# A gating layer's ungated half by seven block products instead of eight, with the block sums made by accumulating loads

## The chip, the core and the metric

The kernel runs on one core of one Trainium2 chip. The metric is the device time of one execution in microseconds (us). TensorE (PE in the profile) multiplies matrices and transposes tiles, VectorE (DVE) and ScalarE (ACT) do element-wise work, GpSimd (POOL) does a little of it. Transfers between the large memory and the on-chip memory (SBUF) are issued from queues: the one of SyncE (SP), the one of ACT, and the one of POOL. Matmul results land in eight accumulation banks (PSUM).

## The reference

Two layers work on a stream `x` of 512 tokens x 1024 features. Layer 0 mixes tokens by chunked attention, layer 1 by a spatial gating layer; each is followed by a feed-forward block of width 4096. All of it is in float32. The part that the change is about is layer 1's mixer:

```python
SG_FF = 6 * D_MODEL          # D_MODEL = 1024
SG_HALF = SG_FF // 2         # 3072
SG_GROUPS, SG_WINDOW, CHUNK = 8, 128, 64

def chunked_spatial_gating(h, w_in, v_gain, w_s, b_s, w_out):
    B, S, _ = h.shape
    nw = S // SG_WINDOW
    z = jax.nn.gelu(h @ w_in, approximate=False)
    u, v = jnp.split(z, 2, axis=-1)
    v = rms_norm(v, v_gain).reshape(B, nw, SG_WINDOW, SG_GROUPS, SG_HALF // SG_GROUPS)
    chunk_id = jnp.arange(SG_WINDOW) // CHUNK
    mask = chunk_id[:, None] >= chunk_id[None, :]
    w = jnp.where(mask[None], w_s, 0.0).astype(v.dtype)
    vm = jnp.einsum('gij,bnjgc->bnigc', w, v) + b_s.T[None, None, :, :, None]
    return (u * vm.reshape(B, S, SG_HALF)) @ w_out

def squared_relu_mlp(h, w1, w2):
    return jnp.square(jax.nn.relu(h @ w1)) @ w2

# per layer: x = x + g1 * mixer(norm(x)); x = x + g2 * squared_relu_mlp(norm(x), w1, w2)
```

In the text `v` is the gated half's input to the mixing ("gate"), `u` the ungated half, and `w_out` the closing product.

## The kernel before

**Products in three passes.** Every float32 operand is split into a high and a low part in a reduced format (`Split`, `wload`: ACT copies the high part, DVE subtracts it for the low part), and `mm3` multiplies high by high, high by low, low by high. So a product over 128 rows of the contraction, 128 tokens and 512 columns takes three matmuls of 128x512.

**Seven products.** `seven(left, src, y)` multiplies a 512 x 1024 activation by a 1024 x 1024 weight as two by two blocks with seven block products instead of eight. Each of its seven steps has four parts: `load` (weight blocks by SP), `right` (the weight blocks' sums on DVE in `sub`, at line 631, and the splits), `left` (sums of activation blocks on DVE, `comb`, and their split) and `mult` (the matmuls, 2 token tiles x 4 k x 3 for one block product; sums over products stay in the accumulation banks or go through `y.put`). `Spent` frees the activation operands after use; `Kept` keeps them for several products in a row. `Run` executes a list of such steps, loads `ll + lp` steps and splits `lp` steps ahead of the matmuls. It is used in the feed-forward layers (`down_steps` there, three of four quarters) and for two thirds of the gate (`Gate(1)`, `Gate(2)`).

**The gating layer, in order.** The first third of the gate is done plainly by `gate_tile` (column blocks 0 and 1, eight products), the rest by two sevens. Each block of v after its Gelu is written to a buffer `vd` in large memory by POOL's queue (`v_store`), and its sums of squares go to `vss`. Then the mixing weights are transposed (line 1495), and `u_block(cb)` runs for six blocks of 512 columns of the ungated half: for each of four token tiles 8 k x 3 matmuls, the Gelu out of the bank, then the mixing of that tile: v is read back, scaled by row scale and gain (L1533), split (L1535, L1536), mixed by two groups' weights (`mm3`, 128 to 384 columns each), biased and multiplied into u (L1549), transposed (L1554) and split again (L1559, L1560). `b_down` multiplies each gated block of 512 columns by its rows of `w_out` and sums in `y` (`Sum`); the last two blocks go through `project_last`, which also adds the residual.

**The last projection.** `project_last` works tile by tile: `merge(t)` scales the sum so far by g and adds the residual that was loaded from `xsg` (L505 to L507); two halves of 512 columns are multiplied; `add_residual` (L424, L425) adds each; `rows(t)` norms the row tile (L304 to L306); `cols(t - 1)`, in the middle of the next tile's second half, transposes the normed tile (L315) for the feed-forward layer. `merge(t)` for t > 0 is issued behind the norm of the tile before (`issue_after(normed[0].ins)`).

**Order.** Outside stretches under `in_order`, which keep PE's instructions as written, a planner orders each engine's instructions by costs of its own. Buffers come from a pool of 49 slots (`Slots`), taken in the order in which they were freed; a load into a slot waits for its last reader. Background work (`bg`) adds up the modulation rows for later stages on DVE from weights loaded on SP.

Of the kernel before, what the change touches and what calls it, by code (L numbers as in the profile page):

```python
# [16 lines left out]
P = 128  # L17
# [35 lines left out]
def trunk_kernel(  # L53
# [378 lines left out]
    def project_last(actT, src, g, rows, cols=None, after=None, merge=None, spent=None):  # L432
# [3 lines left out]
        ws = [ahead.pop(hf) if hf in ahead else wload(src[:, hf * 512:hf * 512 + 512], n) for hf in range(2)]  # L436
        if after is not None:
            ahead["w"] = after()
        for t in range(NT):
# [3 lines left out]
            for hf in range(2):  # L443
                w = ws[hf][0]
                nc_ = 256 if cols is None and (t, hf) == (NT - 1, 1) else 512
                for c0 in range(0, 512, nc_):
                    ps, pi = bank()
                    if hf == 1 and t > 0 and cols is not None:
                        gemm_tok(actT, w[:n // 2], t, ps, 0, n - 1)
                        cols(t - 1)  # L450
# [11 lines left out]
            if cols is not None:  # L462
                rows(t)

# [24 lines left out]
    class Sum:  # L489
# [5 lines left out]
        def merge(self, xs, g):  # L495
            merged = set()

            def merge(t):
# [4 lines left out]
                xt[t], xid[t] = self.y[t], self.ids[t]  # L503
                raw, done = raw_tile([P, D])
# [7 lines left out]
        def put(self, t, hf, ps):  # L512
# [3 lines left out]
            if (t, hf) in self.seen:  # L516
                V.tensor_tensor(dst, ps, dst, ALU.add)  # L517
# [4 lines left out]
    class Spent:  # L522
# [13 lines left out]
        def prep(self, m):  # L536
            if m == 0:
                self.ab = self.blocks()
            elif m == 2:
                self.ab["x"] = SL.get([P, 4, 256], F32)  # L540
                self.comb("x", (1, 0), (1, 1), ALU.add)
            elif m == 3:
                self.comb("x", "x", (0, 0), ALU.subtract)
            elif m == 4:
                self.comb((0, 1), (0, 1), "x", ALU.subtract)
# [3 lines left out]
            if m == 5:  # L549
                self.also()  # L550
            self.spend(*((), (), (), (), ("x", (0, 1)), ((0, 0), (1, 0)), ((1, 1),))[m])

        def also(self):
            pass
# [4 lines left out]
    class Kept(Spent):  # L559
# [11 lines left out]
        def prep(self, m):  # L571
            if m in self.op:
                return
            self.comb(*{
                2: ("x", (1, 0), (1, 1), ALU.add), 3: ("x", "x", (0, 0), ALU.subtract),
                4: ((0, 1), (0, 1), "x", ALU.subtract), 5: ((0, 0), (0, 0), (1, 0), ALU.subtract),
            }[m])
            self.op[m] = Split(self.ab[("x", "x", (0, 1), (0, 0))[m - 2]][0], [P, 4, 256])
            self.spend(*((), (), ("x", (0, 1)), ((0, 0), (1, 0), (1, 1)))[m - 2])
# [5 lines left out]

        def done(self, m):
            pass

        def only_blocks(self):

            for m in (2, 3, 4, 5):
                self.op.pop(m).free()
            return self.rows()

        def free(self):
            for x in self.op.values():
                x.free()
# [18 lines left out]
    def seven(left, src, y):  # L616
# [3 lines left out]
        def load(i, j):  # L620
            raw[i, j] = []
            for s_ in range(2):
                t, n = SL.get([P, 2, 512], F32)
                r0 = i * 512 + s_ * 256
                SP.dma_start(t, src[r0:r0 + 256, j * 512:j * 512 + 512].rearrange("(k p) n -> p k n", p=P))
                raw[i, j].append((t, n))

        def sub(d, a, b):

            for x, y_, z in zip(raw[d], raw[a], raw[b]):  # L630
                V.tensor_tensor(x[0], y_[0], z[0], ALU.subtract)  # L631

        def drop(*blocks):
            for b in blocks:
                SL.free(*[n for _, n in raw.pop(b)])

        def right(m):
            if m == 2:
                sub((0, 0), (0, 1), (0, 0))
            elif m == 3:  # L640
                sub((0, 0), (1, 1), (0, 0))
            elif m == 5:
                sub((0, 1), (1, 1), (0, 1))
            elif m == 6:
                sub((1, 0), (1, 0), (0, 0))
# [1010 lines left out]
```

## Time and profile before

| | before |
|---|---|
| median of 3 runs (lowest to highest) | 1410.66 us (1408.36 to 1410.92) |
| profiled execution: time | 1412.96 us |
| profiled execution: span of its instructions | 1411.2 us |
| mean granted TensorE clock | 0.993 |
| DMA traffic | 221.51 MB, mean 157 GB/s |
| hardware queues' share of the DMA engines, software queue's (POOL) | 45.9%, 1.1% |

The profile is of one execution. Busy time is the time in which an engine worked on instructions; matmuls are pipelined, so a busy PE need not be at its peak. A row of instructions names line, engine, operation, output and inputs, shape and count, then busy time and mean time of one, then the idle time before them and what ended it. "Landing" is the time from a transfer's issue to its data being there.

### The profile page before, as it was taken

The page shows a single profiled execution, that of the slowest core. Times are in us where ns is not written, and L with a number is a line of the kernel's source. Part 1 is how long each engine was busy: PE and PEld are TensorE (multiplying, and loading weights), DVE is VectorE, ACT ScalarE, POOL GpSimd, SP SyncE. Part 2 cuts the span into 40 slices and gives each one's busy share as a digit, 9 for nine tenths or more (in the row PEclk, how much of TensorE's full clock was granted, in tenths as well). Part 3 has the DMA queues.
Part 4 walks back from the last instruction along what each step waited for, and adds up shares of the span by engine and source line. Part 5 has one row for each costly group of instructions (what it writes and reads, how often), then busy time and mean ns, then how long its engine had stood idle before and what let it go on. Part 6 is the DMA issues. An engine that isn't in the chain of part 4 may idle for free.

```text
span 1411.2 us, 18916 instructions
## 1 busy us (share of the span) xinstructions
PE 1386.7 (98%) x7202; PEld 1185.5 (84%) x7202; DVE 1020.9 (72%) x1493; ACT 713.5 (51%) x1231; POOL 15.7 (1%) x46
## 2 busy tenths in 40 slices
PE   8999999899999999999999999999999999999998
PEld 7898888789888888888888888888889988888887
DVE  6889889676667887776995745665677377776883
ACT  6537567655464544537587443233445355453630
POOL 0000000000000000000000000000000000000000
PEclk8999999999999999999999999999999999999999
DMA  9656466573254361356347434435437225242151
GB/s 373 240 144 211 147 194 173 201 264 110 90 169 144 119 224 60 118 197 252 134 147 254 167 106 164 163 127 164 142 113 269 75 87 182 63 147 90 31 164 60
DMA packets 85627, 221.51 MB, mean 157 GB/s; under 512 B 7960, under 2 KB 9376, under 8 KB 85536
## 3 DMA queue, kind: packets, MB, share of 16 engines
q1 hardware_dynamic: 83808, 214.01, 45.9%
q0 software_dynamic: 1728, 6.29, 1.1%
q8 instruction: 56, 0.92, 0.3%
q14 instruction: 35, 0.29, 0.1%
HBM read 197.21 MB, written 14.68 MB: 150 GB/s over the span
## 4 chain that ended last, share of the span: by engine, by line
PE 88%; DMA 6%; DVE 3%; ACT 2%; issue 1%; SPq 0%; POOL 0%; ACTq 0%; POOLq 0%; DVEq 0%
PE p L92 85%; DMA s<-in_ada_w 2%; DMA s<-in_ffn_w 1%; DMA s<-in_a_w_in 1%; DMA s<-in_a_w_out 1%; DMA s<-s 1%; PE p L1554 1%; PE p L1228 1%; PE p L315 1%; DVE s L484 0%; PE p L1139 0%; PE p L920 0%; DVE s L951 0%; ACT s L483 0%; PE p L207 0%
## 5 line engine op out<-in xcount | busy, mean ns | idle before, releaser
L92 PE MATMUL p<-s,s 128*128 128x512 f32 (+2 forms) x6568 | 1323.8, 361 | 9.5 <-DVE nm L1190 2.7
L92 PEld LDWEIGHTS p<-s,s 128*128 128x128 f32 x6568 | 1109.4, 189 | 196.0 <-DVE nm L1190 4.3
L484 DVE TENSOR_TENSOR s<-s,s 128x1024 fp32r<-128x1024 f32 x234 | 280.5, 1222 | 119.1 <-ACT s L483 56.0
L483 ACT CAST s<-s 128x1024 fp32r<-128x1024 f32 x234 | 241.2, 1051 | 166.0 <-PE p L92 109.9
L389 DVE TENSOR_TENSOR s<-s,s 128x1024 fp32r<-128x1024 f32 x80 | 96.7, 1223 | 62.2 <-ACT s L388 50.7
L388 ACT CAST s<-s 128x1024 fp32r<-128x1024 f32 x80 | 83.4, 1052 | 93.8 <-DMA s<-in_b_w_out 34.1
L631 DVE TENSOR_TENSOR s<-s,s 128x1024 f32<-128x1024 f32 x64 | 77.7, 1222 | 33.0 <-DMA s<-in_ffn_w 32.6
L739 ACT ACTIVATE r<-p 128x512 f32<-128x512 f32 x64 | 38.1, 595 | 116.6 <-PE p L92 116.5
L194 DVE SCALAR_TENSOR_TENSOR s<-s,cs,s 128x1024 f32<-128x1024 f32 x70 | 89.7, 1281 | 8.7 <-DMA s<-in_ada_w 7.7
L517 DVE TENSOR_TENSOR s<-p,s 128x512 f32<-128x512 f32 x104 | 70.4, 686 | 19.2 <-PE p L92 18.0
L745 ACT ACTIVATE s<-r 128x256 f32<-128x256 f32 (+1 forms) x112 | 45.0, 443 | 1.2
L424 DVE TENSOR_TENSOR tr<-p,s 128x512 f32<-128x512 f32 (+1 forms) x33 | 22.0, 671 | 30.6 <-PE p L92 30.2
L1195 ACT ACTIVATE s<-s,nm 128x128 f32<-128x128 f32 (+3 forms) x64 | 36.0, 564 | 7.4 <-DVE nm L1190 5.9
L1559 ACT CAST s<-p 128x256 fp32r<-128x256 f32 x48 | 17.7, 370 | 35.5 <-PE p L1554 27.0
L530 DVE TENSOR_TENSOR s<-s,s 128x1024 f32<-128x1024 f32 x28 | 33.6, 1221 | 1.0 <-PE p L92 0.9
L304 ACT ACTIVATE s<-s 128x512 f32<-128x512 f32 x24 | 15.3, 638 | 36.0 <-DVE s L425 34.9
L1233 DVE TENSOR_TENSOR s<-p,s 128x512 fp32r<-128x512 f32 (+3 forms) x64 | 29.3, 484 | 4.0 <-ACT s L1232 3.6
L1560 DVE TENSOR_TENSOR s<-p,s 128x256 fp32r<-128x256 f32 x48 | 20.1, 419 | 16.3 <-ACT s L1559 16.3
L1190 DVE CUSTOM_DVE_ANT_0 s<-p,s 128x128 f32<-128x128 f32 (+3 forms) x64 | 29.6, 485 | 0.9 <-PE p L92 0.8
L1535 ACT CAST s<-s 128x512 fp32r<-128x512 f32 x24 | 14.8, 621 | 27.8 <-DVE s L1533 12.9
L1228 PE MATMUL p<-ident,s 128*128 128x128 f32 x160 | 24.6, 275 | 4.1 <-ACT sq L1310 2.4
L1232 ACT CAST s<-p 128x512 fp32r<-128x512 f32 (+3 forms) x64 | 25.1, 426 | 6.6 <-PE p L1228 5.5
(141 smaller groups left out, 760.9 us busy)
## 6 DMA issues: line engine op xcount, KB each, us to landing
s<-in_ffn_w SPq DMA_DIRECT2D x128, 512.0 KB, 4.5
s<-in_ada_w SPq DMA_DIRECT2D x96, 512.0 KB, 4.9
s<-in_b_w_in SPq DMA_DIRECT2D x48, 512.0 KB, 5.0
s<-in_b_w_out SPq DMA_DIRECT2D x24, 512.0 KB, 4.8
s<-in_a_w_in SPq DMA_DIRECT2D x22, 512.0 KB, 5.2
s<-s SPq DMA_DIRECT2D x64, 128.0 KB, 3.6
vd<-s POOLq DMA_DIRECT2D x12, 512.0 KB, 3.2
s<-vd SPq DMA_DIRECT2D x12, 512.0 KB, 3.4
```

What stands on the lines that cost most here:

```text
L92: T.matmul(ps, lhsT, rhs, start=start, stop=stop, skip_group_check=more)
L194: V.scalar_tensor_tensor(acc, r, ck, acc, ALU.mult, ALU.add)
L388: A.copy(hi, raw)
L389: engs[len(ids) // 2 % len(engs)].tensor_tensor(lo, raw, f32(hi), ALU.subtract)
L483: A.copy(self.hi, raw)
L484: mark[0] = V.tensor_tensor(self.lo, raw, f32(self.hi), ALU.subtract)
L517: V.tensor_tensor(dst, ps, dst, ALU.add)
L631: V.tensor_tensor(x[0], y_[0], z[0], ALU.subtract)
L739: A.activation(r, ps, AF.Relu)
L745: A.activation(d, v, AF.Square)
L1195: A.activation(pt[it], pt[it], AF.Exp, bias=nm[:, it:it + 1], scale=-1.0, accum_out=sm[:, it:it + 1])
L1228: T.transpose(ps[:, it * P:(it + 1) * P], b["pt"][it][:, jt * P:(jt + 1) * P], ident)
```

## The change

It touches four things.

- **Ungated half.** `u_block` goes. The ungated half becomes three sevens over 1024 columns (`mix_steps`, class `Mix`), which use the kept activation operands of the gate. A finished 128 x 512 piece of u gets its Gelu in `Mix.put`; its mixing is put on a list and issued two half steps later (five for the very first) by `flush`. The gated tiles are gathered in blocks of 512 columns x 256 tokens (`gated`) and split as a whole (`take_parts`).
- **Sums by loads.** The seven products take another set of sums, in which each weight operand is a running sum of blocks: x = B00, then + B01, + B11, + B10, and y = B11, then + B01. A block is loaded by SP; the further ones are added onto it in SBUF by an accumulating load from POOL's queue (`grow`) once the split of the operand before has read it. In gate and ungated half (`apart`) the first operand B00 has a buffer of its own, and x is loaded again and grown early.
- **Half steps.** Each of the seven steps becomes two, over 256 weight rows each. `Run` now looks 4 + 4 half steps ahead (before: 3 + 3 whole steps in the feed-forward layers, 2 + 2 in the gate).
- **Closing product.** `down_steps` in the gating layer multiplies 1024 rows of `w_out` in eight half steps, second 512 rows ahead of the first, four token tiles at a time in four banks. Order: ungated third 0, its closing product, ungated thirds 1 and 2, closing product 1, then the last projection for third 2. There the residual is added by an accumulating load from POOL's queue (`late`).

Besides, `v_store` is issued from ACT's queue, and the mixing weights are prepared ahead of the run.

```diff
-        def put(self, t, hf, ps):
+        def put(self, t, hf, ps, op=ALU.add, whole=True):
...
+                if late:
+                    V.tensor_tensor(xt[t], xt[t], g, ALU.mult)
+                    G.dma_start(xt[t], xs[t], accum_op=ALU.add)
+                    return
                 raw, done = raw_tile([P, D])
                 SP.dma_start(raw, xs[t])
                 V.tensor_tensor(xt[t], xt[t], g, ALU.mult)
...
-    def seven(left, src, y):
+    def seven(left, src, y, apart=False):
...
+        def load(name, i, j, s_):
+            raw[name, s_] = t, n = SL.get([P, 2, 512], F32)
+            SP.dma_start(t, block(i, j, s_))
+
+        def grow(i, j, name, s_):
+            G.dma_start(raw[name, s_][0], block(i, j, s_), accum_op=ALU.add)
+
+        def right(m, name, add, s_):
+            t, n = raw[name, s_]
+            op[m, s_] = Split(t, [P, 2, 512])
+            if add is None:
+                SL.free(n)
+            else:
+                grow(*add, name, s_)
...
         plan = (
-            (True, ((0, 0),), False),
-            (True, ((0, 0),), True),
-            (True, ((1, 1),), False),
-            (False, ((0, 1),), False),
-            (False, ((0, 1),), True),
-            (False, ((1, 0), (1, 1)), True),
-            (True, ((1, 0),), True),
+            (0, ("f" if apart else "x", 0, 0), ("f", None) if apart else ("x", (0, 1)), ("z", True, ((0, 0, add, False),), False)),
+            (1, ("z", 1, 0), ("z", None), ("y", True, ((0, 0, add, False),), True)),
+            (2, None, ("x", (1, 1)), ("v", True, ((1, 1, add, False),), False)),
+            (4, ("y", 1, 1), ("y", (0, 1)), ("v", False, ((0, 1, add, False),), True)),
+            (3, None, ("x", (1, 0)), ("z", False, ((0, 1, sub, False),), False)),
+            (5, None, ("y", None), ("z", False, ((1, 1, sub, False),), False)),
+            (6, None, ("x", None), ("z", False, ((1, 0, add, True),), True)),
         )
-        blocks = ((0, 0), (1, 0), (0, 1), (1, 1))
+        def loads(m, b, s_):
+            if b:
+                load(*b, s_)
+            if apart and m == 1:
+                load("x", 0, 0, s_)
+                grow(0, 1, "x", s_)
...
-        run = Run(steps, 3, 3)
+        run = Run(steps, 4, 4)
...
-        G.dma_start(vd[cb, b], v.rearrange("p t n -> p (t n)"))
+        A.dma_start(vd[cb, b], v.rearrange("p t n -> p (t n)"))
...
+        def put(self, t, hf, ps, op, whole):
+            if (hf, t // 2) not in self.u:
+                self.u[hf, t // 2] = SL.get([P, 2, 512], F32)
+            dst = self.u[hf, t // 2][0][:, t % 2, :]
+            if not whole and (t, hf) not in self.seen:
+                self.seen.add((t, hf))
+                A.copy(dst, ps)
+                return
+            if not whole:
+                V.tensor_tensor(dst, dst, ps, op)
+            A.activation(dst, ps if whole else dst, AF.Gelu)
+            late = 5 if (self.p, hf, t // 2) == (0, 0, 0) else 2
+            later.append((now[0] + late, lambda: self.mix(t, hf, dst)))
...
+        def mult(n):
+            hf, j, o = n // 4, 1 - n // 2 % 2, n % 2
+            w = op.pop(n)
+            for t in range(NT):
+                if n % 4 == 0:
+                    ps[t] = bank()
+                a = parts[p, t // 2, j]
+                c = slice(t % 2 * P, t % 2 * P + P)
+                for k in range(2):
+                    kk = 2 * o + k
+                    mm3(
+                        ps[t][0], a.hi[:, kk, c], a.lo[:, kk, c], w.hi[:, k, :], w.lo[:, k, :],
+                        n % 4 == 0 and k == 0, n % 4 == 3 and k == 1,
+                    )
+                if n % 4 == 3:
+                    y.put(t, hf, ps[t][0])
+                    PS.free(ps[t][1])
...
+    steps += u[0] + d[0] + u[1] + u[2] + d[1][:6] + tail + d[1][6:]
+    run = Run(steps, 4, 4)
+    run.prime()
+    for t in range(NT):
+        gate_tile(1, t, ws[1][0])
...
-    u_block(0)
-    u_block(1)
-    b_down([0])
-    u_block(2)
-    b_down([1])
...
-    b_down([4, 5])
+    project_last(
+        plain({(i, j): parts[2, i, j] for i in range(2) for j in range(2)}), b_w_out[0][2048:3072, :], g,
+        last.rows, last.cols, lambda: up_ahead(1), y.merge(xs, g, True), spent
+    )
```

More of the change, by code (lines that the diff above doesn't have):

```diff
@@ L584, in comb @@
             super().comb(d, a, b, o)
+        more = True
         def done(self, m):
[L587 to L597, printed above, removed]
+            if not self.more:
+                super().done(m)
     def plain(p):
@@ L683, in seven @@
             )
-            for m in range(7)
+            for m, b, r, p in plan for s_ in range(2)
         ]
@@ L722, in up_ahead, with ffn @@
         return [up_split(up_load(l, 0, n)) for n in range(4)]
-    def ffn(l, norm, rows, cols, after, bgn):
+    def ffn(l, norm, rows, cols, after, bgn, lag=1):
         h = norm.h
```

352 lines of the change are left out of this document (186 added, 166 removed).

## The prediction

> **What bounds the kernel now.** I read the page's busy list first, then busy time by stage, then the chain that ended last inside single stages.
>
> ```profile
> span 1411.2 us, 18916 instructions
> PE 1386.7 (98%) x7202; PEld 1185.5 (84%) x7202; DVE 1020.9 (72%) x1493; ACT 713.5 (51%) x1231; POOL 15.7 (1%) x46
> ```
>
> PE idles 1411.2 - 1386.7 = 24.5 us in all. The stages say where; the columns are length, then PE, weight loads, DVE, ACT, POOL, granted clock, DMA share and GB/s.
>
> ```profile
> 663.00:771.00 108.00, 108.00 (x482) 89.36 (x480) 88.36 (x85) 75.31 (x129) 6.57 (x13) 1.00 0.48 163
> 693.00:770.00 77.00, 77.00 (x341) 63.68 (x340) 62.63 (x63) 59.07 (x96) 4.86 (x10) 1.00 0.54 181
> 771.00:1020.00 249.00, 249.00 (x1204) 208.91 (x1203) 155.07 (x240) 92.92 (x149) 0.53 (x1) 1.00 0.45 151
> 1020.00:1083.00 63.00, 61.22 (x338) 52.66 (x336) 46.99 (x81) 31.09 (x66) 0.00 (x0) 1.00 0.59 205
> 1083.00:1411.20 328.20, 324.42 (x1590) 275.29 (x1588) 213.26 (x217) 142.22 (x197) 0.00 (x0) 1.00 0.31 101
> ```
>
> From the gate (693 to 770, ungated half and its closing product to 1020, last projection to 1083) PE is idle for 1.8 us only, at full granted clock, while DVE, ACT and DMA have room. So this stage is worth what its matmuls cost, as long as nothing else becomes late. The chain of work gives the price of a matmul, and of one token tile of the ungated half.
>
> ```profile
> 645.99 13.62 PE p L92 x60
> 865.09 0.47 PE p L92 x2
> 865.88 5.88 PE p L92 x28
> 871.87 0.46 PE p L92 x2
> ```
>
> A 128x512 matmul takes 13.62 / 60 = 0.227 us. A token tile of `u_block` takes 871.87 - 865.09 = 6.78 us: 24 matmuls (5.45) and 1.33 of mixing and transposes.
>
> **The change, part by part.** *Seven products for eight.* Before, the ungated half is 6 column blocks x 4 tiles x 8 k x 3 = 576 matmuls. After, it is 3 x 7 products x 2 tiles x 4 k x 3 = 504. 72 fewer x 0.227 = **16.3 us** off PE, in a stage where PE is never idle. Mixing, transposes, the closing product (576 before, 2 x 192 + 192 after) and the sevens elsewhere keep their counts; half steps only cut the same matmuls into groups of 12 (2.72 us).
>
> *DVE and ACT.* These rows carry the prices.
>
> ```profile
> L631 DVE TENSOR_TENSOR s<-s,s 128x1024 f32<-128x1024 f32 x64 | 77.7, 1222 | 33.0 <-DMA s<-in_ffn_w 32.6
> L484 DVE TENSOR_TENSOR s<-s,s 128x1024 fp32r<-128x1024 f32 x45 | 54.3, 1223 | 17.4 <-ACT s L483 12.8 <-DMA vd<-s 4.4
> L483 ACT CAST s<-s 128x1024 fp32r<-128x1024 f32 x43 | 44.3, 1054 | 20.3 <-DMA s<-in_ffn_w 10.4 <-PE p L92 4.7 <-PE p L207 1.9
> L517 DVE TENSOR_TENSOR s<-p,s 128x512 f32<-128x512 f32 x24 | 16.2, 685 | 5.2 <-PE p L92 5.2
> L1533 DVE SCALAR_TENSOR_TENSOR s<-s,vr,gain 128x512 f32<-128x512 f32 x24 | 17.6, 748 | 14.5 <-PE p L92 11.1 <-issue 1.4 <-PE p L1554 1.1
> L1536 DVE TENSOR_TENSOR s<-s,s 128x512 fp32r<-128x512 f32 x24 | 16.3, 687 | 1.9 <-ACT s L1535 1.7
> L1549 DVE SCALAR_TENSOR_TENSOR s<-p,bsT,s 128x256 f32<-128x256 f32 x16 | 7.0, 479 | 1.0 <-PE p L92 0.8
> ```
>
> The 64 weight sums (77.7 us of DVE) go altogether; PE was 100% busy beside them, so I count nothing for it. One ungated seven now asks of DVE: 14 splits x 1.223 = 17.1, six adds into SBUF x 0.685 = 4.1, eight mixings x (0.748 + 0.687 + 2 x 0.479) = 19.1, and in the third seven four splits of gated blocks, 4.9: 45.2 us. PE takes 168 x 0.227 + 8 x 1.33 = 48.8 us. DVE stays behind PE, with 3.6 us to spare in the tightest seven; were that cover gone, the excess would go to PE one for one. ACT has less: its 14 casts are 14.8 us, and copies and Gelus at most about as much as the mixing on DVE. The closing half steps ask 8 x 1.223 of DVE in 43.6 us, beside at most nine sums for the modulation rows. Nothing counted.
>
> *Sums by loads.* Each seven now issues 8 accumulating loads of 512 KB from POOL, and 6 plain ones from SP (8 in gate and ungated half, where it was 8). An accumulating load reads its target too; no row of this trace has one. The nearest rows are plain loads, and stores from SBUF on the POOL queue; the first fence is 640 to 660, where DMA is saturated, the second 693 to 770, the last line the store's landing over the whole run.
>
> ```profile
> q1 hardware_dynamic: 2988, 6.83, 92.3%
> s<-in_b_w_in SPq DMA_DIRECT2D x9, 512.0 KB, 7.4
> ...
> q0 software_dynamic: 1008, 3.67, 11.8%
> s<-in_b_w_in SPq DMA_DIRECT2D x16, 512.0 KB, 5.0
> ...
> DMA to landing us min/median/max: 2.9/3.2/7.6
> ```
>
> Latency: at least a Pool transfer, 3.2 us; at most a crowded load and the slowest Pool transfer in a row, 7.4 + 7.6 = 15.0. I take load plus read-back, 5.0 + 3.2 = **8.2 us**, because the operation is those two movements and the DMA share of these stages is about half. In engine time a load costs 0.923 x 20 x 16 / 6.83 = 43 us per MB, SBUF traffic 0.118 x 77 x 16 / 3.67 = 40, so an accumulating load 83.
>
> Gate, per seven: 4.2 MB x 43 + 4.2 x 83 + 2.1 MB of stores x 40 = 613 engine us / 16 = 38.3 us, against PE's 168 x 0.227 = 38.1. Just covered, since the first eight half steps' loads go out 21.8 us ahead. Ungated: 2.1 MB of gate loads and 0.5 of gains in place of the stores, 39.6 of 48.8 us. In the feed-forward layers the added 3.1 MB per seven lie beside 360 matmuls (81.7 us), DMA at 0.31: nothing.
>
> The sums also form a chain: split (1.05 + 1.22), accumulate, split, four half steps (10.9 us) apart, and each operand is ready four half steps ahead. Two links may slip by 10.9 - 2.3 = 8.6 us together: they fit when 2 x (2.3 + L) is at most 21.8 + 8.6, so L up to 12.9 us. At 8.2 nothing is late; at 15.0 a gate seven loses 4.2 us, the two 8.4. I take 0, keep 8.4.
>
> *Moved queues.* The gate stores go from POOL to ACT: POOL's queue now holds accumulating loads, each waiting for its split on DVE, and a store would stand behind them. ACT pays the issue (12 x about 0.35 us, estimated from an SP issue below). The mixing weights are transposed before the run instead of behind it, the same eight transposes; row scales now come from DVE steps, five half steps (13.6 us) ahead of the first mixing: nothing.
>
> *The last projection.* Here a wait is added. Before, the residual is loaded early and added by two DVE steps (L506, L507). After, the product is scaled, then an accumulating load adds the residual, and only then can `add_residual` run. The scaling is issued behind the previous tile's norm. The DVE's and PE's rows:
>
> ```profile
> 1037.92 0.75 DVE L306 TENSOR_SCALAR s<-s,ru 128x1024 f32<-128x1024 f32 x1
> 1038.59 1.22 DVE L506 TENSOR_TENSOR s<-s,s 128x1024 f32<-128x1024 f32 x1
> 1041.71 1.04 PE L315 MATMUL p<-ident,s 128*128 128x128 f32 x8
> 1042.82 0.32 SPq L505 DMA_DIRECT2D s<-xsg  x1
> 1046.61 0.68 DVE L425 TENSOR_TENSOR s<-s,tr 128x512 f32<-128x512 f32 x1
> 1049.02 0.75 DVE L306 TENSOR_SCALAR s<-s,ru 128x1024 f32<-128x1024 f32 x1
> 1053.52 1.03 PE L315 MATMUL p<-ident,s 128*128 128x128 f32 x8
> 1082.13 1.06 PE L315 MATMUL p<-ident,s 128*128 128x128 f32 x8 [1.55 <-DVE s L306]
> ```
>
> From a norm's end to the next: 1.22 (scale) + L + 2 x 0.69 + 2.48 (1047.29 to 1049.77) = 5.1 + L. PE spends 1053.52 - 1041.71 = 11.8 us per tile, and the first norm is 1041.71 - 1038.67 = 3.0 us early. With L = 8.2 the chain is 13.3 and loses 1.5 us per tile: the norms of tiles 1 and 2 end at 1052.0 and 1065.2, just in time; tile 3's at 1038.7 + 3 x 13.3 = 1078.6, ahead of the 1080.6 at which PE was ready for it. Loading was heavy there (1.55 us idle already), so I add **2 us**. At L = 3.2 nothing, at 15.0 it is 1038.7 + 3 x 20.1 - 1080.6 = 18.4 us.
>
> Collectives: The Full Stack in the Trainium skill, part 3 on the bandwidth ceiling, speaks against the change: an add in the DMA engine "needs two source reads" on one ring, so it runs at half a copy's rate. No run here has shown it. Applied to the load row it would make L 10.0 instead of 8.2; the projection then ends 3 x 15.1 - 41.9 = 3.4 us late, and the sum would be 1.4 us higher than mine.
>
> *Sum.* The profiled execution took 1412.96 us, 1.8 outside its span and 2.3 above the runs' median, 1410.66. 1412.96 - 16.3 + 2.0 = 1398.7 in its terms; against the median, 1396.4.
>
> **Rivals.** *Slower: the residual's accumulating load in the last projection.* By the sum above its cost is 3 x L - 26.6 us. It eats the whole 16.3 from L = 14.3 us on. For it: the chain is serial, DMA share 0.59 there, and plain transfers have taken 7.4 to 7.6 us under load. Against it: two of the three links fall in quiet stretches. At L = 17 it gives 1410.7 - 16.3 + 24.4 = 1419.
>
> *Some of the gain is given back:* L between 9.5 and 13. The projection loses 2 to 12 us, the gate's chains none: 1396 to 1407, at L = 11 some 1401. The page's factor two falls here.
>
> *Loads bind in the gate.* If an accumulating load cost three plain ones, a gate seven would need (4.2 x 43 + 4.2 x 129 + 84) / 16 = 50.4 us, 12.3 more than PE, twice; an ungated one 51.7, 2.9 more, three times: 33 us, less the 21.8 us lead. Net 11 us back: 1406. The saturated stretch that still moves 6.83 MB in 20 us speaks against a price so high.
>
> *No change:* it needs give-backs of 13.5 to 19 us, L about 13.5 to 15, or DVE queueing behind late sums in the third ungated seven, where it has 3.6 us to spare.
>
> **How the numbers follow.** 0.2% (2.8 us) is about what a measurement of this kernel can tell from no change. The forecast (nothing late but 2 us; 1391 to 1401) gets 0.55. Gain partly given back, by projection or gate, 1401 to 1408: 0.17. No change: 0.08. Slower: 0.20, since every sum hangs on a DMA that the trace doesn't show. Hence faster 0.72, same 0.08, slower 0.20. Below: all PE idling of these stages gone (1.8 us) and nothing given back is 1410.7 - 18.1 = 1392.6, and 1391 with the runs' spread. The range goes from 1391 to 1417, leaving out most of the slower case.
>
> **What would show it.** Right: PE busy about 16 us less, at 1370; stage windows at 100% PE; the weight sums of DVE gone, some 90 accumulating loads on POOL landing in 6 to 10 us. Wrong: PE idle ahead of matmuls released by splits, with splits released by POOL's loads; or PE idle ahead of the transposes of the norm (L315 here), with `add_residual` waiting for the residual's load; or landing times beyond 13 us.

## The result: slower by 1.6%

| | before | after |
|---|---|---|
| median (lowest to highest), four runs each | 1409.51 us (1404.87 to 1410.92) | 1431.05 us (1429.06 to 1433.84) |
| ratio to before, 95% interval | | 1.016 [1.013, 1.019] |
| profiled execution: time, span | 1412.96, 1411.2 us | 1431.17, 1429.4 us |
| mean granted TensorE clock | 0.993 | 0.985 |

The forecast was 1396.4 us. The kernel became 21.5 us slower, beyond the end of the range (1417). First the busy list of the profile after:

```profile
span 1429.4 us, 18936 instructions
PE 1378.3 (96%) x7130; PEld 1175.6 (82%) x7130; DVE 955.0 (67%) x1402; ACT 743.1 (52%) x1248; POOL 119.8 (8%) x126
```

72 matmuls are gone (7202 - 7130), as the change says; at the prediction's price they are worth 16.3 us. But PE is busy only 8.4 us less (1386.7 to 1378.3), and it idles 51.1 us (1429.4 - 1378.3) instead of 24.5. So the 18.2 us between the two profiled spans are -16.3 (matmuls) + 26.6 (idle) + 7.9 (what is left: PE busy longer than the count of matmuls says). The stages say where. First two stretches of the kernel before, then the kernel after; columns as in the prediction (length, PE, weight loads, DVE, ACT, POOL, clock, DMA share, GB/s).

```profile
660.00:820.00 160.00, 160.00 (x741) 133.22 (x740) 124.83 (x148) 100.90 (x172) 7.13 (x14) 1.00 0.49 169
820.00:1010.00 190.00, 190.00 (x912) 159.22 (x911) 111.98 (x162) 65.02 (x101) 0.00 (x0) 1.00 0.43 143
```

```profile
300.00:660.00 360.00, 360.00 (x1803) 306.70 (x1803) 237.35 (x270) 183.47 (x287) 31.41 (x26) 1.00 0.67 188
660.00:820.00 160.00, 139.36 (x582) 112.59 (x581) 83.64 (x95) 86.50 (x142) 27.29 (x24) 0.94 0.83 213
820.00:1010.00 190.00, 183.15 (x899) 153.12 (x899) 132.90 (x180) 102.36 (x143) 19.32 (x16) 0.99 0.71 195
1010.00:1110.00 100.00, 99.08 (x541) 85.71 (x540) 71.26 (x111) 45.67 (x83) 5.09 (x5) 1.00 0.61 187
1110.00:1390.00 280.00, 280.00 (x1339) 236.25 (x1338) 167.00 (x160) 137.59 (x186) 27.67 (x23) 1.00 0.57 139
```

All of the new idle time lies between 660 and 1010 us, in the two sevens of the gate and the ungated half: 20.6 + 6.9 = 27.5 us, where there was none. The granted clock also falls there, to 0.94 and 0.99 (1.00 in both stretches before). The feed-forward stages, with the same accumulating loads, stay at 100%. DMA is fuller but not full. The waits of PE and ACT in the kernel after (total, times, longest):

```profile
PE p L92 <- ACT s L1542: 11.0, 2, 8.5
PE p L92 <- DVE s L1427: 5.1, 2, 3.2
PE p L92 <- DVE s L486: 3.7, 1, 3.7
PE p L92 <- ACT s L485: 3.3, 2, 3.1
...
ACT s L485 <- DMA s<-in_b_w_in: 69.0, 20, 10.4
```

L485 and L486 are the split, L1542 is the copy of a bank in `Mix.put`, L1427 the sum out of a bank in `Gate.put`. All four rows of PE lie between 660 and 1010 us. Only 7.0 us of PE's waiting ended on a split itself; 16.1 us ended on a copy or a sum out of a bank. The loads, from the DMA part:

```profile
q0 software_dynamic: 24512, 48.24, 20.4%
...
s<-in_ffn_w POOLq DMA_DIRECT2D x48, 512.0 KB, 5.9
...
s<-in_b_w_in POOLq DMA_DIRECT2D x40, 512.0 KB, 8.9
...
s<-xsg POOLq DMA_DIRECT2D x4, 512.0 KB, 6.1
```

An accumulating load landed in 8.9 us in these stages (8.2 predicted) and in 5.9 in the feed-forward layers. It took 0.204 x 16 x 1429.4 / 48.24 = 97 engine us per MB (83 predicted): the time of the DMA engines, added over all 16, for one MB of POOL's loads. Neither is far off, and yet the stage loses. Rows picked from the timeline (start, length, engine, in brackets the idle time before and its releaser) show the way from a load to PE:

```profile
784.00 1.05 ACT L485 CAST s<-s 128x1024 fp32r<-128x1024 f32 x1 [7.92 <-DMA s<-in_b_w_in]
785.08 2.36 DVE L486 TENSOR_TENSOR s<-s,s 128x1024 fp32r<-128x1024 f32 x2 [10.42 <-ACT s L485]
786.61 2.44 POOL L625 DMA_DIRECT2D s<-in_b_w_in  x2 [12.06 <-DVE s L486]
787.36 0.68 DVE L1427 TENSOR_TENSOR s<-s,p 128x512 f32<-128x512 f32 x1
788.09 19.62 PE L92 MATMUL p<-s,s 128*128 128x512 f32 x78 [3.22 <-DVE s L1427]
796.60 2.95 ACT L485 CAST s<-s 128x1024 fp32r<-128x1024 f32 x3 [5.38 <-DMA s<-in_b_w_in]
799.21 3.71 POOL L625 DMA_DIRECT2D s<-in_b_w_in  x3 [8.29 <-DVE s L486]
814.58 1.04 ACT L485 CAST s<-s 128x1024 fp32r<-128x1024 f32 x1 [10.41 <-DMA s<-in_b_w_in]
815.53 1.06 ACT L1542 COPY s<-p 128x512 f32<-128x512 f32 x2
816.16 13.21 PE L92 MATMUL p<-s,s 128*128 128x512 f32 x53 [8.45 <-ACT s L1542]
```

A split frees its operand, and POOL issues the next additions in a burst of two, later in one of three. The splits that wait for loads start 12.6 and 18.0 us after the one before. The prediction had 2.3 + 8.2 = 10.5 for such a link. The loads of a burst land one behind the other: the three issued from 799.21 on took 6.8, 10.2 and 12.8 us from issue to landing, and the third, landed at 814.56, released the split at 814.58. PE had stopped at 788.09 + 19.62 = 807.71, so the bank that L1542 copies was full by then; the copy started only at 815.53, right behind the late split on ACT. The sum at 787.36 stands in the same way behind two late splits on DVE. So in these two waits, 11.7 of the 27.4 us that PE waits between 660 and 1010 us, it waits for work that stands behind a split, and not for the split's own operand.

### The profile page after: what moved, and what is told of

It is laid out like the page before. It is cut to its first block, busy times and chain, and to the rows that moved or that the text cites. A ratio compares the mean times of both kernels' runs of the same rounds, so it can differ in the third digit from the quotient of the medians.

```text
span 1429.4 us, 18936 instructions
## 1 busy us (share of the span) xinstructions
PE 1378.3 (96%) x7130; PEld 1175.6 (82%) x7130; DVE 955.0 (67%) x1402; ACT 743.1 (52%) x1248; POOL 119.8 (8%) x126
## 3 DMA queue, kind: packets, MB, share of 16 engines
q0 software_dynamic: 24512, 48.24, 20.4%
## 5 line engine op out<-in xcount | busy, mean ns | idle before, releaser
L486 DVE TENSOR_TENSOR s<-s,s 128x1024 fp32r<-128x1024 f32 x304 | 366.9, 1223 | 285.1 <-ACT s L485 227.1
L485 ACT CAST s<-s 128x1024 fp32r<-128x1024 f32 x304 | 313.1, 1050 | 235.1 <-PE p L92 100.8
L625 POOL DMA_DIRECT2D s<-in_ffn_w x48 | 58.3, 1214 | 498.2 <-DVE s L486 395.1
L625 POOL DMA_DIRECT2D s<-in_b_w_in x40 | 48.4, 1246 | 316.1 <-DMA s<-in_b_w_in 180.9
L388 ACT CAST s<-s 128x1024 fp32r<-128x1024 f32 x40 | 41.7, 1052 | 49.4 <-DMA s<-in_ffn_w 19.2
L523 DVE TENSOR_TENSOR s<-s,p 128x512 f32<-128x512 f32 x76 | 50.2, 683 | 15.5 <-PE p L92 15.2
L389 DVE TENSOR_TENSOR s<-s,s 128x1024 fp32r<-128x1024 f32 x40 | 48.1, 1223 | 16.1 <-ACT s L388 15.8
L536 DVE TENSOR_TENSOR s<-s,s 128x1024 f32<-128x1024 f32 x28 | 33.7, 1223 | 10.9 <-PE p L92 10.5
L319 ACT ACTIVATE tt<-p,mod,mod 128x128 f32<-128x128 f32 x64 | 24.0, 462 | 21.0 <-PE p L315 10.5
L425 DVE TENSOR_TENSOR s<-s,tr 128x512 f32<-128x512 f32 (+1 forms) x33 | 22.2, 674 | 15.0 <-DMA s<-xsg 14.4
```

The costliest lines, as they stand in the source:

```text
L388: A.copy(hi, raw)
L389: engs[len(ids) // 2 % len(engs)].tensor_tensor(lo, raw, f32(hi), ALU.subtract)
L485: A.copy(self.hi, raw)
L486: mark[0] = V.tensor_tensor(self.lo, raw, f32(self.hi), ALU.subtract)
L523: V.tensor_tensor(dst, dst, ps, op)
L536: V.tensor_tensor(self.ab[d][0], self.ab[a][0], self.ab[b][0], o)
```

## The experiments

All are edits of the kernel after; engine us per MB are over all 92 loads of POOL's queue, and the residual's four of these still accumulate where the sevens' loads are plain. In the first run, the accumulating loads of the sevens only load.

```diff
-            G.dma_start(raw[name, s_][0], block(i, j, s_), accum_op=ALU.add)
+            G.dma_start(raw[name, s_][0], block(i, j, s_))
```

> The changed kernel, but POOL's accumulating loads in the seven products are plain loads from the same queue, at the same places, with the same waits: the addition of the weight blocks is left out. Theory A (the price of the accumulation: the transfer reads its target too, so each link of split, add, split takes too long): landing on POOL falls from some 7 to 9 us to 4 to 6 us, the PE idling between 700 and 1000 us (27 us, and some 8 us of slowed matmuls) mostly goes, and the time comes to 1398 to 1406 us. Theory B (the sums start late: SP's plain load waits for a buffer that PE frees, and POOL's queue stands behind that load in order, whatever it does then): landing falls too, but the idling stays, 1422 to 1432 us. By the factor two of a rule that an add needs two reads, the engine time per MB on the software queue should fall from 97 to about 48.

1403.85 us, ratio to before 0.996 [0.995, 0.997]. Every engine has the same instructions in the same order as in the kernel after. The queue and landing rows, and the two stages:

```profile
q0 software_dynamic: 13248, 48.24, 11.3%
...
s<-in_b_w_in POOLq DMA_DIRECT2D x40, 512.0 KB, 5.7
```

```profile
660.00:820.00 160.00, 155.55 (x701) 128.05 (x701) 104.01 (x127) 102.44 (x167) 16.53 (x24) 0.99 0.68 230
820.00:1010.00 190.00, 188.18 (x913) 157.49 (x912) 137.55 (x170) 101.49 (x135) 11.59 (x16) 1.00 0.62 207
```

So theory A holds, and 27 us are the price of accumulating itself: same bytes, same order, about half the packets, 0.113 x 16 x 1401.6 / 48.24 = 53 engine us per MB and 3.2 us less to landing. The second run brings the sums back, on DVE, from blocks that SP loads once.

```diff
+                    V.tensor_tensor(t, t, raw[other, s_][0], ALU.add)
...
-    run = Run(steps, 4, 4)
+    run = Run(steps, 3, 3)
```

> The changed kernel with the weight sums of gate and ungated half made by DVE again (8 additions of 128x1024 per seven, from blocks loaded once by SP), in the feed-forward layers still by accumulating loads; look-ahead 3 + 3 half steps in place of 4 + 4, for lack of buffers. Theories A and B both: PE no longer waits for POOL, and the gain of 72 matmuls comes out, less what DVE now lacks: an ungated seven asks 45 + 9.8 = 55 us of DVE against 48.8 of PE, so up to 6 us late three times, partly caught up in the closing products: 1396 to 1412 us. Theory C (the half steps, the order and the mixing two half steps later are the trouble, not the sums): idling stays with PE waiting for ACT and DVE, 1420 us or more.

1401.92 us, 0.994 [0.992, 0.996]: faster than both kernels. The rest of the change is in it, but for the look-ahead (3 + 3) and the operand with a buffer of its own. So theory C, that half steps, order and late mixing are the trouble, is out. The stages:

```profile
660.00:820.00 160.00, 157.58 (x728) 130.47 (x727) 132.92 (x156) 103.59 (x165) 0.61 (x2) 1.00 0.47 157
820.00:1010.00 190.00, 189.02 (x907) 157.46 (x906) 158.00 (x189) 98.58 (x130) 0.90 (x1) 1.00 0.49 162
```

Only the gate's sums on DVE (`Gate(p), True, V`, the ungated half as in the kernel after):

> The changed kernel with the weight sums on DVE in the two sevens of the gate only; the ungated half still by accumulating loads. In the changed kernel PE idles some 20 us between 700 and 820 us, where the gate's sums run, and some 6 us later; matmuls run slowed after such gaps. Theory A and B: most of the gate's loss goes, 1405 to 1415 us, what is left lies in the ungated half. If the loss only moves to the ungated half (its first seven starts as crowded as the gate did): 1418 to 1428 us.

1420.31 us, 1.007 [1.005, 1.010], on the side of the loss that moves on: PE 148.52 of 160 and 183.79 of 190 us. The ungated half's first accumulating loads are issued while the gate still runs: 8 of the 24 go out between 746 and 799 us, and the gate's last sum of squares ends at 799. So the cure of the gate alone gave 1431.1 - 1420.3 = 10.7 us, about a third of the second run's 29. Without `apart` (`Gate(p))` and `m)` in place of `Gate(p), True)` and `m, True)`):

> The changed kernel without the separate first operand in gate and ungated half: x is loaded once, split for the first product and then grown three times, as in the feed-forward layers; 14 transfers per seven in place of 16, of which 8 accumulate as before. Theory A (chain of links, each about 10 us with its split): one link more in the same time, slower than the changed kernel, 1435 to 1450 us. Theory B (start of the chain late because of the second load of x, and too many transfers in the queue): x comes eight half steps ahead and POOL no longer waits for it, faster than the changed kernel, 1410 to 1425 us.

1433.55 us, 1.017 [1.014, 1.019], as the kernel after, between the two expectations: the operand with a buffer of its own and the early reload neither help nor harm, as far as these runs can tell. What of the accumulating load is it, then: its length, or the engines' time? First plain loads with one copy of 512 KB in large memory for each:

```diff
+            SP.dma_start(dump[copies[0] % 8], src[...])
```

> As e1 (plain loads on POOL in place of accumulating ones, the addition of the weight blocks left out), and with each of them one more transfer of 512 KB that nothing waits for: a copy of the same weight block to a spare buffer in large memory, issued by SP. It puts back engine time of about the size of the read-back (some 48 us per MB estimated from the plain loads) without lengthening any link. Theory A1 (the transfer engines are full: DMA share was 0.83 between 660 and 820 us and reached 1.08 in single stretches): the idling comes back, 1418 to 1432 us. Theory A2 (a link is too long, the engines have room): as e1, 1402 to 1408 us.

1466.88 us, and it tells nothing: the planner issued the copies early, DMA was at 0.94 in the first 300 us and PE lost its time there. Then plain loads with a second transfer of 64 KB behind each, into the same buffer (a longer link):

```diff
+            G.dma_start(raw[name, s_][0][:, 0:1, 0:128], block(i, j, s_)[:, 0:1, 0:128])
```

> As e1 (plain loads on POOL, the addition left out), but each is followed on the same queue by a second transfer of 64 KB into the same buffer, which must wait until the first has landed; the split then waits for both. It lengthens each link by 2.5 to 3.5 us, about as much as the accumulation did (landing 8.9 against 5.7 us), with an eighth more traffic. Theory A2 (length of the links): the idling comes back, 1415 to 1432 us. Theory A1 (engines full): 1402 to 1410 us. POOL's queue is also held while the second waits, so a time above the changed kernel's would speak for the queue's order rather than the landing.

1417.56 us, 1.006 [1.004, 1.007]: 13.7 us more than the plain loads, at the same DMA share.

```profile
660.00:820.00 160.00, 146.84 (x643) 118.52 (x642) 94.94 (x112) 94.03 (x153) 28.56 (x46) 0.99 0.68 228
```

With sums on GpSimd (the second run with `G.tensor_tensor`):

> As e2, but the weight sums of gate and ungated half are additions on GpSimd instead of DVE: DVE keeps 45 of 48.8 us per ungated seven as forecast, GpSimd gets 8 additions of 128x1024. The Trainium skill's GPSIMD Engine Reference puts an addition of two inputs at about twice DVE's time, an estimate of 2.2 to 2.4 us here. If they run beside DVE's work: 1394 to 1401 us, a few us better than e2. If the additions hold up DVE (both read two inputs from SBUF) or take over 4 us: 1402 to 1412 us.

1422.88 us, 1.009 [1.008, 1.011], beyond both expectations. Rows of its groups (busy, mean ns of one):

```profile
L486 DVE TENSOR_TENSOR s<-s,s 128x1024 fp32r<-128x1024 f32 x304 | 395.9, 1321 | 218.4 <-ACT s L485 166.1 <-PE p L92 36.9 <-DMA vd<-s 5.7
L636 POOL TENSOR_TENSOR s<-s,s 128x1024 f32<-128x1024 f32 x40 | 112.3, 2812 | 286.0 <-DVE s L486 256.5 <-ACT s L1554 21.9 <-issue 4.5
```

An addition took 2.81 us there (1.22 on DVE), and DVE's own subtractions rose to 1.32 us over the whole run (1.22 in the kernel after). SBUF — State Buffer in the Trainium skill says, under its two separate sides, that a DVE operation with two inputs in SBUF and a GpSimd operation that reads SBUF shut each other out of a shared pair of ports; the longer subtractions agree with that, but no run here shows the ports. The second run with the residual loaded plainly (`y.merge(xs, g)`):

> As e2, with the residual of the last projection loaded plainly by SP and added on DVE, as before the change. My forecast gave the accumulating residual 2 us (landing 8.2 us) and its rival 16 or more (landing over 14 us). In the changed kernel its landing is 6.1 us and PE idles 0.9 us ahead of the norm's transposes. Theory of the forecast: within 2 us of e2, 1399 to 1403 us. The rival (the residual's load decides): 1385 to 1395 us.

1400.08 us, 0.994 [0.992, 0.995]: 1.8 us below the second run, within the noise of the two (their intervals overlap). So no cost of the last projection's accumulating load is shown beyond a few us, and the rival's 16 or more are ruled out. This is also the best version, level with the second run. The copies again, now tied behind the block's load on SP:

```diff
+            with tc.issue_after(loaded[0].ins):
+                loaded[0] = SP.dma_start(dump[copies[0] % 8], src[...])
```

> As e5 (plain loads on POOL, the addition left out, one copy of 512 KB per load from large memory to large memory that nothing waits for), with the copies held behind the weight loads of their step on SP's queue: in e5 the planner had put most of them ahead, into the first 300 us, where they held up another stage. Between 660 and 820 us the DMA share should be about that of the changed kernel, 0.8 to 0.9, against 0.68 in e1. Theory A1 (engines full): the idling comes back, 1418 to 1432 us, with landings of 8 us and more on POOL. Theory A2 (length of the links): 1402 to 1410 us. If both have a part, between: 1410 to 1418 us, which with e6's 1418 would share the changed kernel's 27 us over e1 about evenly.

1408.31 us, 0.999 [0.998, 1.001], 4.5 us more than the plain loads. DMA is fuller than in the kernel after (0.87 to 0.83), and PE hardly notices:

```profile
660.00:820.00 160.00, 153.56 (x689) 125.82 (x688) 103.74 (x125) 102.16 (x167) 16.50 (x24) 0.99 0.87 306
...
s<-in_b_w_in POOLq DMA_DIRECT2D x40, 512.0 KB, 7.5
```

But the loads land later too, in 7.5 us against 5.7, and the copies gave every engine but POOL another order (some 385 of PE's instructions stand elsewhere than in the first run). So this run doesn't part full engines from long links: here both together cost 4.5 us.

Two tries to count slack link by link: one accumulating load less per chain (the second addition to `x` made by DVE from `y`), and the kernel after with the second run's look-ahead.

```diff
+            elif apart and (name, add) == ("x", (1, 1)):
+                V.tensor_tensor(t, t, raw["y", s_][0], ALU.add)
```

> The changed kernel, but in gate and ungated half the second of x's three additions (block 11, which lies in SBUF as y) is made by DVE; six accumulating loads per seven in place of eight, and x's chain loses its middle link. DVE pays 2 x 1.22 us per seven. Theory A2 (links): the two links left have 8 half steps of room instead of two links in four each, 1402 to 1414 us. Theory A1 (engines full): a quarter of the accumulating traffic goes, 2.1 of 16.7 MB-equivalents, 1418 to 1426 us.

1427.6 us, 1.012 [1.009, 1.014].

> The changed kernel with a look-ahead of 3 + 3 half steps in the gating layer instead of 4 + 4 (the one that e2 had to use); nothing else is changed. Operands are split 8.2 us ahead instead of 10.9. Theory A2: each chain has 2.7 us less slack, more idling in each of five sevens, 1440 to 1460 us. Theory A1: the demand is the same, 1428 to 1436 us. If it is not slower than the changed kernel, e2's gain cannot be laid to its look-ahead either way.

1425.25 us, 1.010 [1.009, 1.012], some 6 us less than with 4 + 4. Both missed: the loss goes neither simply by the number of links nor by how early the first one starts. In the kernel after the shorter look-ahead is worth some 6 of the second run's 29 us; what it is worth there wasn't tried. Last of the sums, those of the feed-forward layers on DVE as well:

> As e2, with the weight sums of the feed-forward layers on DVE as well, so that no seven uses an accumulating load. My forecast counted nothing for those in the feed-forward layers (PE 100% busy there with and without them). Same as e2: 1398 to 1404 us. If the accumulating loads cost something there too, 1390 to 1397 us.

1402.42 us, 0.993 [0.990, 0.995], as the second run: the sums by loads in the feed-forward layers cost nothing and bring nothing that these runs can tell. Then the longer link and the tied copies in one kernel:

> The changed kernel with every accumulating load of the sevens replaced by a plain load of the same 512 KB (so the sums are left out), followed on the same queue by a plain load of 64 KB into the same buffer (a longer link), and with one more 512 KB copy in large memory, issued by SP behind the block's load, for each of them (full DMA engines). The longer link alone cost 13.7 us over plain loads (1417.6 against 1403.9), the copies alone 4.5 (1408.3). Theory 1, the two are late in different places and only add up: 1403.9 + 13.7 + 4.5 = 1422, 1418 to 1425; then some 9 us of the changed kernel's loss are something else of the accumulating load (its burst behind one another, its issue of 1.20 us). Theory 2, length and load act on one another, since a longer link that also queues misses its half step: 1426 to 1438, and the changed kernel's 1431 is explained by these two. In both, idle PE between 660 and 1010 us, ahead of matmuls released by ACT's and DVE's splits, more than the 13.2 us that the longer link alone left between 660 and 820.

1423.2 us, 1.0105 [1.008, 1.013]: the two only add up, and 8 us of the 27 stay. But these kernels' second transfers also change the order that the planner writes. So a slower transfer without a second one: plain loads cut into pieces of 512 or 256 bytes (same number of bytes, out of other rows of the weight), and the same loads accumulating. In each pair all engines have the same order; with 512 bytes some matmuls stand elsewhere than in the kernel after, with 256 bytes clearly more.

```diff
+            G.dma_start(raw[name, s_][0].rearrange("p k n -> p (k n)").rearrange("p (c n) -> p c n", c=8),
+                flat(src, j * 512 + i * 256 + s_ * 128, [[src.ap[0][0], P], [src.ap[0][0] * 128, 8], [1, 128]]))
```

> The changed kernel with every accumulating load of the sevens replaced by one plain load of 512 KB that is cut into pieces of 512 bytes, out of other rows of the same weight (so the sums are left out and other weights are multiplied): a plain transfer that takes the engines longer, with no second transfer behind it and nearly the same order of instructions. Theory 1, the price and the landing time of the transfer by themselves make the loss: the time lies on a line between plain loads in long pieces (1403.9; 52 engine us per MB, landing 5.7 us) and the changed kernel (1431; 97, 8.9), by where this load's price lies between the two: at 75 engine us per MB some 1417. Theory 2, some 8 us of the loss belong to the accumulating load in another way: the line ends at 1423, and at 75 it is 1413.

> The same with pieces of 256 bytes, a still slower plain load. Theory 1: where its price is 97 engine us per MB and its landing 8.9 us, 1426 to 1436, as the changed kernel; where both are above, more than that. Theory 2: 1418 to 1425 at that price. Both: PE idle ahead of matmuls released by the splits between 660 and 1010 us, and the feed-forward layers (300 to 660 us) at 360 us of PE.

> The plain load in pieces of 256 bytes landed in 8.6 us, almost the 8.9 of the changed kernel's accumulating load, and lost nothing (1409.5 us). But the planner knew of its length: it wrote the matmuls, splits and adds in another order than in the changed kernel, whereas it gave accumulating and plain loads of long pieces the same order on every engine. This run has that kernel's instructions in exactly the same order, and the loads in pieces of 256 bytes are accumulating ones (of other rows, so the sums are of the wrong weight). Theory P, the loss comes of an order planned for loads of 5 to 6 us: with an order planned for 8 to 9 us the same accumulating loads cost little, 1408 to 1418 us at a landing of 9 to 10 us, PE above 150 of 160 us between 660 and 820. Theory A, the loss lies in the accumulating loads whatever the order (their queueing, their share of the engines): 1424 to 1440. If the landing is above 11 us, the short pieces have made the accumulation dearer, and a time above 1424 tells nothing.

> The same with pieces of 512 bytes, against the plain load in such pieces (1415.5 us, landing 6.7), again in exactly its order, which is nearly that of the changed kernel. Theory P: the order fits loads of 6 to 7 us no better than the changed kernel's, 1424 to 1436. Theory A: the same, 1424 to 1440. It is the pair of the run before: if the two differ by over 8 us at about the same landing time, the order makes the difference.

Queue and landing rows of the four, in this order:

```profile
q0 software_dynamic: 13248, 48.24, 12.1%
...
s<-in_b_w_in POOLq DMA_DIRECT2D x40, 512.0 KB, 6.7
```

```profile
q0 software_dynamic: 13248, 48.24, 14.2%
...
s<-in_b_w_in POOLq DMA_DIRECT2D x40, 512.0 KB, 8.6
```

```profile
q0 software_dynamic: 182208, 48.24, 37.2%
...
s<-in_b_w_in POOLq DMA_DIRECT2D x40, 512.0 KB, 13.4
```

```profile
q0 software_dynamic: 92096, 48.24, 26.6%
...
s<-in_b_w_in POOLq DMA_DIRECT2D x40, 512.0 KB, 10.7
```

Engine time is worked out as above, from share and span (1412.9, 1405.5, 1441.9, 1443.9 us).

| kernel | order planned as | landing us | engine us per MB | time us | ratio, interval |
|---|---|---|---|---|---|
| plain, long pieces | after | 5.7 | 53 | 1403.9 | 0.996 [0.995, 0.997] |
| plain, 512 B | nearly after | 6.7 | 57 | 1415.5 | 1.005 [1.004, 1.007] |
| after: accumulating | after | 8.9 | 97 | 1431.1 | 1.016 [1.013, 1.019] |
| accumulating, 512 B | nearly after | 10.7 | 127 | 1447.2 | 1.027 [1.025, 1.030] |
| plain, 256 B | for longer loads | 8.6 | 66 | 1409.5 | 1.000 [0.999, 1.002] |
| accumulating, 256 B | for longer loads | 13.4 | 178 | 1443.7 | 1.025 [1.023, 1.027] |

Pair by pair, accumulating costs 27, 32 and 34 us more than a plain load in the same order. In the first four rows, whose order is the same or nearly so, the time rises with the landing by (1447.2 - 1403.9) / (10.7 - 5.7) = 8.7 us for each us, and the two rows between lie within 3 us of that line. There is no flat part between 5.7 and 6.7 us: the plain load in pieces of 512 bytes, with 1 us of landing more, took 11.6 us more. By engine time the same rows fit worse: a line from 53 to 97 engine us per MB puts 57 at 1407, and 1415.5 was measured. That points to the time of the link and not to the engines' time. It doesn't part landing from POOL's time to issue, which rises along with it over the four rows (0.72, 0.88, 1.25, 1.65 us).

The line holds for this order alone. In the other order, that of the last two rows, a landing of 8.6 us costs 1409.5 where the line gives 1429, and one of 13.4 costs no more than 10.7 does in the first. The tied copies (7.5 us, 1408.3; line 1419), the kernel without `apart` (8.4, 1433.6; line 1427) and the look-ahead of 3 + 3 (9.5, 1425.3; line 1437) have orders of their own, and lie off the line on both sides. So landing by itself doesn't settle the time. The two plain loads in pieces were cheaper than their expectations supposed (57 and 66 engine us per MB, not 75 and 97). The strong form of theory P, that an order planned for such loads cures the accumulating ones, isn't shown: in pieces of 256 bytes they landed at 13.4, not 9 to 10 us, and by the expectation's own bound their time decides nothing on it. The accumulating load in pieces of 512 bytes also overshot its range by 7 us. What stays open is why one order bears 2 to 3 us more than the other, and how the 8.7 us per us is made up of single waits.

## Why the prediction was wrong

**The step that failed** is the one that priced the chains of sums: "Two links may slip by 10.9 - 2.3 = 8.6 us together ... At 8.2 nothing is late ... I take 0". Nothing late was forecast for these chains, and 27 us were measured. The step took the slack from the arithmetic of half steps and gave all of it to the loads. In the order that PE, ACT and DVE were given, that slack isn't there: with the 5.7 us of a plain load PE already idles for 4.4 us between 660 and 820 us (2.4 with the sums on DVE), and from there each further us costs 8.7 in this order. By that line, L = 8.2 is 2.5 us past the plain load and costs 22 us. Two parts of the link were left out. The additions are issued in bursts and land one behind the other (12.6 and 18.0 us a link in the chain shown, not 10.5). And a split that waits holds up what stands behind it on ACT and DVE, bank copies and sums that PE needs at once; so a late split costs long before its own operand is due. That is shown for the two waits of PE above (8.5 and 3.2 us), not for each. The "8.4" kept for these chains, at the worst L of 15.0, had the same flaw: the loss came to three times that at 8.9 us.

**"Just covered" in the gate.** 38.3 engine us against 38.1 of PE per seven left no room, but a full DMA was not enough to bind: with 0.87 of the engines busy, plain loads lost 4.5 us, in an order of their own. (The 39.6 us of an ungated seven reads the gate's loads at the stores' 40 us per MB; at the loads' 43 it is 40.1, which changes nothing.) The rival *loads bind in the gate* (1406) named the right place with the wrong limit.

**Sizes of the load.** 8.2 us against 8.9, and 83 engine us per MB against 97: both near, the bounds 3.2 to 15.0 held. Collectives: The Full Stack in the Trainium skill says in part 3, of the adds in collectives, that an add in the DMA engine needs two source reads and so runs at half a copy's rate; the traces come near it for long pieces, 97 / 53 = 1.8, and show more for short ones, 127 / 57 = 2.2 and 178 / 66 = 2.7. The prediction had that page's L at 10.0, and let it cost only 1.4 us, by the same flat step.

**The matmuls.** The count of 72 was right. The 16.3 us come out in the profiled executions only: with the sums on DVE, PE is busy for 1369.2 us (1370 predicted), idles 27.5 instead of 24.5, and the span is 1396.7, 14.5 below before. But that execution was one of the fastest of its runs (1398.47, median 1401.92), and the one of before one of the slower (1412.96, median 1409.51). By medians the second run is 7.7 us faster than before, 5 to 11 by its interval, and the one with the plain residual 8.9. So about half of the 16.3 us shows, even where no seven of the gate or the ungated half accumulates by loads; where the rest stays is open. In the kernel after PE was busy 7.9 us longer than the count says, in stretches with a granted clock of 0.94 and 0.99. Part of that can be spread: with all sums on DVE and no such gaps, one execution had PE busy for 1375.4 us.

**The last projection.** 2 us were taken; the medians show 1.8 (1401.92 against 1400.08), which the noise doesn't part from nothing. The rival that carried the "slower" chance, the residual's load beyond 14.3 us, did not happen: it landed in 6.1.

**DVE, feed-forward sums, moved queues.** Nothing was counted, and the runs show nothing. DVE stayed behind PE (132.90 of 190 us busy between 820 and 1010 us), even with the sums back on it (158.00); the 3.6 us to spare in the tightest seven were not measured by themselves. The feed-forward stages are at 100% of PE with either kind of sum: the 360 matmuls beside a seven were the cover named, and there the loads landed in 5.9 us. The store on ACT's queue shows in one wait of 2.4 us of a subtraction on DVE (`DVE s L486 <- DMA vd<-s: 2.4, 1, 2.4`), in none of PE.

## What to carry to other kernels

A load that is moved into a chain (split, load, split) can't be priced against the slack that a count of steps promises. Ask what stands behind the waiting instruction on its engine, and who needs that at once: where a planner laid the order for shorter loads, the slack may be zero. A price per us of landing is that of one order, and doesn't carry over to the next. Replacing an addition by a transfer can pay only where no engine has room for the addition: here DVE had it, and 27 us were paid to free it. The same edit can be free in one stage (feed-forward, 82 us of matmuls per seven) and dear in another (gate, 38 us), so each stage is asked by itself.

## What the runs showed of the hardware

An accumulating load of 512 KB on POOL's queue took 1.8 times the engine time of a plain one (97 to 53 us per MB), nearly twice the packets (24512 to 13248 in all), and 1.25 us of POOL to issue (0.72); in pieces of 256 bytes 2.24 us (1.15) and 2.7 times. Cutting a plain load into pieces of 512 bytes cost little engine time (57 to 53 us per MB), and yet 1 us of landing. Additions on GpSimd took 2.3 times as long as on DVE (2.81 to 1.22 us); DVE's own subtractions of that size took 1.52 us between 660 and 1010 us in that run, 1.32 over the whole of it, against 1.22. A stretch of 160 us in which PE stood still five times, for 1.9 to 8.5 us, had a granted clock of 0.94, where the same stretch had 1.00 before and 0.99 with plain loads.
